# Order of the work where an output product hands over to the first gate product

## The chip, the cores and the metric

The kernel runs on one core of a Trainium2 chip. A core has five engines with queues of their own: TensorE (PE, matrix products; its weight loads are shown as PEld), VectorE (DVE), ScalarE (ACT), GpSimd (POOL) and SyncE (SP, which here issues most DMAs). PE, DVE, ACT and POOL each take their instructions in the order in which they were queued. The metric is the device time of one execution in microseconds (us), the median of several runs; lower is better.

## The reference

A trunk of two layers over 1024 tokens of width 1024, all in float32. Layer 0 mixes tokens by attention, layer 1 by a gated recurrence; each layer ends with a SwiGLU feed-forward block of inner width 2816. Every sub-layer is `x = x + RMSNorm(f(RMSNorm(x)))`. Cut to what matters here:

```python
def rmsnorm(x, g):
    y = x * rsqrt(mean(x * x, axis=-1) + 1e-6)
    return y * g

for layer in range(2):
    m = mixer(rmsnorm(x, norm_mix_pre[layer]))            # ends with ... @ w_out
    x = x + rmsnorm(m, norm_mix_post[layer])
    h = rmsnorm(x, norm_ffn_pre[layer])
    f = (silu(h @ w_gate) * (h @ w_up)) @ w_down
    x = x + rmsnorm(f, norm_ffn_post[layer])
```

The place of this study is the passage from `@ w_out` over the two norms to the first columns of `h @ w_gate`. It comes twice, once in each layer; the text calls each a joint.

## The kernel before, in words

**Precision.** A float32 operand is split into a rounded part (hi, written by a cast on ACT) and the rest (lo, a subtraction on DVE); a product is three matmuls, hi·hi, hi·lo and lo·hi.

**Output product** (`out_product`, matmuls on L602). The 1024 tokens are eight tiles of 128. Tiles 0 to 2 are accumulated together, then 3 to 5, then 6 and 7. When the sums of a tile are complete in PSUM, its norm follows (`norm`, `post_norm_of`, `rstd`, `pre_norm`):

- ACT squares and sums the tile (L179), POOL makes the factor of the norm in two one-column operations (L183 adds the epsilon, L184 is the power -1/2), DVE multiplies by the gain (L251, which reads PSUM) and adds the residual (L257).
- Of the new x, ACT takes the squares again (L179), POOL makes the second factor (L183, L184), and ACT scales (L213). That last instruction is called `scaled` in the code.
- PE turns the scaled tile: eight 128x128 transposes (L223) into two PSUM banks.

**The turned tile** is taken by `HiddenS.take`: ACT copies both banks to SBUF (L85). The feed-forward products go by Strassen's scheme in Winograd's form, seven products in place of eight, so their right-hand operands are seven blocks: three of the turned tile itself and four differences `tf`. They are kept in three groups: the first has two blocks (operands 0 and 1), the second one block (operand 2), the third the four differences (operands 3 to 6). Each group is cast by ACT (L96, hi) and subtracted by DVE (lo); all DVE operations of `take` go through one helper and show as L89. There is one buffer for `tf`.

**The first gate product** (`first`, `strassen`, matmuls on L759 to L761). Tiles 0 to 3 are turned well before tiles 6 and 7 are normed. So the first 256 columns of the first gate block (seven products A11, A12, S2, S3, S1, S4, A22 of twelve 256-column matmuls each) are computed from tiles 0 to 3 while tiles 6 and 7 are normed and turned. The operands of A11 and A12 are those of the first group, S4's that of the second, the others are of the third. `strassen` is a generator: `out_product` takes the products up to a yield, queues a tile's transposes behind the last matmul so far, and the rest of the products behind the transposes (`hold`). Then the late half, columns 256 to 512, needs tiles 4 to 7. L765 to L776 add the products up as they come out of PSUM.

**Its weights** (`gate_load`): the loads (L714), a scaling by the norm's gain on ACT (L717), then sums and differences on DVE (L736 to L738, L743), and for each of the seven a cast on ACT (L729) and a lo part on DVE (L730). S3, S1, the difference L743 and S4 are under `self.behind(behind)`.

**What sets the order.** `self.behind([i, ...])` queues the instructions traced in its block behind instruction i, if they run on i's engine; it adds no wait between engines. For the rest, the program builder plans the order on each queue from dependencies, from the order in which the code issues the instructions, and from a timing of its own; then data dependencies become waits on semaphores.

Of the kernel before, what the change touches and what calls it, by code (L numbers as in the profile page):

```python
# [8 lines left out]
F32 = mybir.dt.float32  # L9
# [27 lines left out]
class HiddenT:  # L37
# [7 lines left out]
    def take(self, t, pst, scratch, pool):  # L45
        nc = self.nc
        if isinstance(t, tuple):
            r, a = t
            hh, hl = (h.rearrange("p k (a t r i) -> p k a t r i", a=2, t=2, r=2)[:, :, a % 2, :, r, :]
                      for h in self.half[a // 2])  # L50
            pst = [ps.rearrange("p a (t i) -> p a t i", t=2) for ps in pst]
        else:
            tok = slice((t % 4) * P, (t % 4) * P + P)
            hh, hl = (h[:, :, tok] for h in self.half[t // 4])
        for q, ps in enumerate(pst):
            hi = hh[:, 4 * q:4 * q + 4]
            self.last = nc.scalar.copy(hi, ps).ins
            self.last_lo = nc.vector.tensor_tensor(
                hl[:, 4 * q:4 * q + 4], ps, hi.bitcast(F32), op=ALU.subtract).ins


class HiddenS:
# [18 lines left out]
    def take(self, t, pst, scratch, pool):  # L81
        nc = self.nc
        hf = scratch.rearrange("p (q a b) -> p q a b", q=2, a=4)
        for q, ps in enumerate(pst):
            nc.scalar.copy(hf[:, q], ps)  # L85
        lo, hi = slice(0, 64), slice(64, P)
        b11, b12, b21, b22 = hf[:, 0, :, lo], hf[:, 0, :, hi], hf[:, 1, :, lo], hf[:, 1, :, hi]
        tf = pool.tile([P, 4, 4, 64], F32, tag="tf", bufs=1, name=self.uid("tf"))
        sub = lambda o, x, y: nc.vector.tensor_tensor(o, x, y, op=ALU.subtract)  # L89
        sub(tf[:, 0], b12, b11)  # L90
        sub(tf[:, 2], b22, b12)
        sub(tf[:, 1], b22, tf[:, 0])
        sub(tf[:, 3], tf[:, 1], b21)
        cols = slice(64 * t, 64 * t + 64)
        for src, (h, l) in zip((hf[:, :, :, lo], hf[:, 1:2, :, hi], tf), self.g):
            self.last = nc.scalar.copy(h[:, :, :, cols], src).ins  # L96
            self.last_lo = sub(l[:, :, :, cols], src, h[:, :, :, cols].bitcast(F32)).ins


class Trunk:  # L100
# [165 lines left out]
    def attention(self, x_src, xT_src, w_v, w_qk, bias_t, o_dst, hT, pools, open_first):  # L266
        nc, tc = self.nc, self.tc
        with ExitStack() as ctx:
# [255 lines left out]
            for q in range(2):  # L524
                wv.append(self.split(None, 4, 256, raw=raws[q]))
                for c in range(2):
                    take(c, (q,))
                    for tt in range(2):
                        v_part(banks[2 * c + tt], wv, 2 * c + tt, range(4 * q, 4 * q + 4))
            squares(0); squares(1)  # L530
            evacuate(vt, 0)
            take(2)
            v_tile(grp, wv, vt, 2)
            squares(2); squares(3)
            evacuate(vt, 1)
            take(3)
            v_tile(grp, wv, vt, 3)
            spread(0)
# [34 lines left out]
    def psum(self):  # L573
        return self.pp.tile([P, 512], F32, tag="mm", bufs=6, name=self.uid("ps"))
# [4 lines left out]
    def out_product(self, ap, pp, first, aT, w, x_src, x_dst, gpost_v, sink, kts):  # L579

        nc = self.nc
# [16 lines left out]
        def matmuls(ps, passes, first, last):  # L598

            for n in range(2):  # L600
                for i, (x, y) in enumerate(passes):
                    self.matmul = nc.tensor.matmul(ps[:, n * 512:(n + 1) * 512], x, y[:, n, :], start=first and i == 0,  # L602
                                     stop=last and i == len(passes) - 1).ins

        def norm(t, ps):
            mg = ap.tile([P, D], F32, tag="mg", bufs=3, name=self.uid("mg"))

            x = self.apool.tile([P, 1152], F32, tag="first", name=self.uid("x"))[:, :D] if t in (2, 5) else None
            return self.post_norm_of([(slice(0, D), ps)], mg, x_src, x_dst, t, gpost, sink, ap, x)
# [6 lines left out]
        for t0 in (0, 3):  # L616
# [30 lines left out]
            last_m = self.last_m  # L647
# [27 lines left out]
        for t in range(2):  # L675
            for i in range(4):

                with self.behind([self.matmul] + ([self.turned[3 + i]] if t == 0 and i < 3 else [])):
                    matmuls(pst[t], [(acts[i][:, t * P:(t + 1) * P], rows[i])], False, i == 3)
            if t == 0:  # L680
                rest = norm(6, pst[0])
                last_m = self.last_m
                turn6 = rest(True)
                squared, summed = self.squared, self.summed


        last, products, hold = first([*last_m, summed], psum)
        with self.behind([squared]):
            rest = norm(7, pst[1])
        last_m = self.last_m  # L690
# [56 lines left out]
    def strassen(self, hS, psum, c, q, cols, behind=()):  # L747

        nc = self.nc
        s1, u2, u3, c22 = c

        def product(name, i):
            ps, a = psum(), q[name]
            for kt in range(4):
                bh, bl = hS.op(i, 0, kt, cols), hS.op(i, 1, kt, cols)
                with self.behind(behind):
                    nc.tensor.matmul(ps, a[:, 0, kt, :], bh, start=kt == 0, stop=False)  # L759
                nc.tensor.matmul(ps, a[:, 0, kt, :], bl, start=False, stop=False)  # L760
                self.matmul = nc.tensor.matmul(ps, a[:, 1, kt, :], bh, start=False, stop=kt == 3).ins  # L761
            return ps

        tt = nc.vector.tensor_tensor
        nc.scalar.copy(s1, product("A11", 0))  # L765
        yield self.matmul
        p2 = product("A12", 1)
        tt(u2, product("S2", 4), s1, op=ALU.add)
        tt(s1, p2, s1, op=ALU.add)
        tt(u3, product("S3", 5), u2, op=ALU.add)  # L770
        p5 = product("S1", 3)
        tt(u2, p5, u2, op=ALU.add)
        yield self.matmul
        tt(c22, p5, u3, op=ALU.add)
        tt(u2, product("S4", 2), u2, op=ALU.add)
        tt(u3, u3, product("A22", 6), op=ALU.subtract)  # L776

    def gate_up(self, ap, hS, early, wg, wu, gain, gO):
# [17 lines left out]
        for j in range(NF // 2):  # L796
            if j == 0:
                cg = blocks()
                strassen([o[:, late] for o in cg], q, late)
                for i, o in enumerate(cg):  # L800
                    nc.scalar.activation(o[:, early], first[:, i], AF.Silu)
                    nc.scalar.activation(o[:, late], o[:, late], AF.Silu)
            else:
                q = self.gate_load(ap, wg, gain, j, ["w"] * 7, self.last if j == 1 else None)
                cg = blocks()
                strassen(cg, q, full)
                for o in cg:
                    nc.scalar.activation(o, o, AF.Silu)
            qu = self.gate_load(ap, wu, gain, j, ["w"] + ["w2"] * 6, hS.last if j == 0 else None)
            cu = blocks()  # L810
            strassen(cu, qu, full)
            for o, u in zip(cg, cu):
                tt(o, u, o, op=ALU.mult)
            a11, a21, a12, a22 = cg
            s1, s2, s4, _ = cu
            tt(s1, a21, a22, op=ALU.add)
            tt(a21, a11, a21, op=ALU.subtract)
            tt(s2, s1, a11, op=ALU.subtract)
            tt(s4, a12, s2, op=ALU.subtract)
            for name, o in (("A11", a11), ("S2", s2), ("S3", a21), ("S1", s1), ("A22", a22),  # L820
                            ("S4", s4), ("A12", a12)):
                nc.sync.dma_start(gO[name][:, j] if name == "A12" else gO[name][j], o)
# [464 lines left out]
```

## Time and profile before

| | us |
|---|---|
| median of 3 runs | 2181.53 |
| lowest and highest of them | 2178.12, 2184.14 |
| the profiled execution, its own time | 2188.6 |
| its span, first to last instruction | 2186.8 |

Mean granted PE clock in the profiled execution: 0.996 of full speed. The two joints lie at about 572 to 599 us and 1540 to 1568 us of the span.

How to read the rows: in a timeline a row is the start, the length, the engine, the line of the code, the operation, output<-inputs with their shape, and in brackets how long the engine had stood idle before and what released it. Rows of several equal instructions are merged (x8). In a view of waits a row is the waiting engine, tile and line, what it waited for, us in total, number of times and the longest. In a view of windows a row gives the length of the window, then busy us with the number of instructions for PE, PEld, DVE, ACT and POOL, then the granted clock, the DMA share and GB/s. SPq is SyncE's queue. Buffer names: `ps` sums in PSUM, `mg` and `x` the tile in its norm, `pst` the transposes, `hS` the groups, `q` and `raw` gate or up weights, `rs` and `ss` the norm's factor and its sum.

### The profile page before, as it was taken

Reading aid. Unit: us, or ns where it says so; the run is one execution under the profiler, and the core shown is the slowest. Engines: PE = TensorE matmul, PEld = TensorE weight load, DVE = VectorE, ACT = ScalarE, POOL = GpSimd, SP = SyncE. Lnnn points to the kernel's source line nnn. Section 1 sums busy time; section 2 is a strip of 40 time slices with the busy share of each in tenths; the row PEclk is TensorE's granted clock in tenths of the full one; section 3 lists DMA queues with packets and bytes.
Section 4 is the critical chain, followed back from the end, with each engine's and each line's share of the span. In section 5 each row is a group of like instructions: output and inputs, shape, how many; then the busy total and the mean of one; then the engine's idle time right before and its main releaser. Section 6 shows DMA issues by size and latency. Waiting matters only on the chain.

```text
span 2186.8 us, 30432 instructions
## 1 busy us (share of the span) xinstructions
PE 2158.0 (99%) x11140; PEld 1803.8 (82%) x11140; DVE 1500.0 (69%) x2458; ACT 1173.2 (54%) x2174; POOL 220.4 (10%) x398
## 2 busy tenths in 40 slices
PE   9999999999999999999999999999999999999998
PEld 8888989878788888888887777887788888888886
DVE  5747555656877677767778667437786767758675
ACT  7656555556755445433446576537755454424452
POOL 2111113121100000000002333102100000000011
PEclk9999999999999999999999999999999999999999
DMA  7111012126334233336467311356133333328565
GB/s 284 44 49 49 30 40 64 43 99 205 133 103 133 92 118 99 106 106 242 136 196 225 98 49 54 95 199 230 63 130 102 121 97 98 110 87 293 169 183 154
DMA packets 167453, 269.42 MB, mean 123 GB/s; under 512 B 13964, under 2 KB 94860, under 8 KB 167304
## 3 DMA queue, kind: packets, MB, share of 16 engines
q1 hardware_dynamic: 166520, 265.38, 37.9%
q10 hardware_dynamic: 784, 2.10, 0.3%
q8 instruction: 87, 1.43, 0.3%
q14 instruction: 62, 0.51, 0.1%
HBM read 199.80 MB, written 65.54 MB: 121 GB/s over the span
## 4 chain that ended last, share of the span: by engine, by line
PE 86%; DVE 5%; ACT 3%; DMA 2%; issue 2%; POOL 1%; SPq 0%; POOLq 0%; DVEq 0%; ACTq 0%
PE ps L760 13%; PE ps L759 13%; PE ps L761 13%; PE ps L602 6%; PE ps L845 5%; PE ps L846 5%; PE ps L844 5%; PE pso L370 3%; PE tr L435 3%; PE psq L167 3%; PE psq L168 2%; PE psq L169 2%; PE ps L168 2%; PE ps L169 2%; PE ps L167 2%
## 5 line engine op out<-in xcount | busy, mean ns | idle before, releaser
L759 PE MATMUL ps<-hS,q 128*128 128x512 f32 (+1 forms) x1288 | 490.4, 381 | 0.0
L760 PE MATMUL ps<-hS,q 128*128 128x512 f32 (+1 forms) x1288 | 489.9, 381 | 0.5 <-DVE hS L89 0.5
L761 PE MATMUL ps<-hS,q 128*128 128x512 f32 (+1 forms) x1288 | 489.2, 380 | 0.0
L730 DVE TENSOR_TENSOR q<-raw,q 128x512 fp32r<-128x512 f32 x308 | 205.6, 688 | 180.7 <-ACT q L729 180.1
L760 PEld LDWEIGHTS ps<-hS,q 128*128 128x128 f32 x1288 | 243.1, 189 | 47.0 <-DVE hS L89 0.9
L761 PEld LDWEIGHTS ps<-hS,q 128*128 128x128 f32 x1288 | 243.0, 189 | 46.1
L759 PEld LDWEIGHTS ps<-hS,q 128*128 128x128 f32 x1288 | 242.7, 189 | 46.1 <-DVE tf L89 0.2
L729 ACT CAST q<-raw 128x512 fp32r<-128x512 f32 x308 | 178.8, 619 | 165.4 <-DVE raw L738 127.6
L845 PE MATMUL ps<-o,o 128*128 128x512 f32 x616 | 240.2, 390 | 0.5 <-DVE o L840 0.4
L846 PE MATMUL ps<-o,o 128*128 128x512 f32 x616 | 237.7, 389 | 0.0
L717 ACT ACTIVATE raw<-raw,gcol 128x256 f32<-128x256 f32 x352 | 150.8, 502 | 138.7 <-DMA raw<-in_ffn_w_up_dram 74.8
L844 PE MATMUL ps<-o,o 128*128 128x512 f32 x616 | 218.6, 390 | 1.8 <-ACT o L839 1.8
L839 ACT CAST o<-raw 128x512 fp32r<-128x512 f32 x173 | 104.2, 622 | 148.3 <-PE ps L846 52.5
L183 POOL TENSOR_SCALAR rs<-ss 128x1 f32<-128x1 f32 x52 | 34.0, 654 | 1416.2 <-ACT junk L179 1344.1
L840 DVE TENSOR_TENSOR o<-raw,o 128x512 fp32r<-128x512 f32 x173 | 116.1, 688 | 53.1 <-ACT o L839 52.6
L844 PEld LDWEIGHTS ps<-o,o 128*128 128x128 f32 x616 | 115.3, 188 | 27.2 <-ACT o L839 3.7
L845 PEld LDWEIGHTS ps<-o,o 128*128 128x128 f32 x616 | 115.6, 188 | 25.6 <-DVE o L840 1.8
L846 PEld LDWEIGHTS ps<-o,o 128*128 128x128 f32 x616 | 115.6, 188 | 24.0
L157 DVE TENSOR_TENSOR wlo<-raw,whi 128x1024 fp32r<-128x1024 f32 x76 | 93.4, 1229 | 58.6 <-ACT whi L156 57.3
L423 DVE TENSOR_TENSOR_SCAN pr<-pr,zero 128x128 f32<-128x128 f32 (+7 forms) x64 | 86.6, 1359 | 51.3 <-POOL pr L420 49.6
L156 ACT CAST whi<-raw 128x1024 fp32r<-128x1024 f32 x76 | 79.8, 1052 | 52.1 <-PE ps L168 23.4
L167 PE MATMUL psq<-hT,whi 128*128 128x512 f32 x256 | 102.4, 400 | 1.2 <-ACT v L310 1.0
(208 smaller groups left out, 4278.6 us busy)
## 6 DMA issues: line engine op xcount, KB each, us to landing
raw<-in_ffn_w_gate_dram SPq DMA_DIRECT2D x44, 512.0 KB, 4.2
raw<-in_ffn_w_up_dram SPq DMA_DIRECT2D x44, 512.0 KB, 4.2
gS<-c SPq DMA_DIRECT2D x88, 256.0 KB, 3.8
raw<-gS SPq DMA_DIRECT2D x88, 256.0 KB, 2.8
gA<-c SPq DMA_DIRECT2D x66, 256.0 KB, 3.4
raw<-gA SPq DMA_DIRECT2D x44, 256.0 KB, 2.7
t<-in_ffn_w_down_dram SPq DMA_DIRECT2D x22, 512.0 KB, 6.5
raw<-in_ffn_w_down_dram SPq DMA_DIRECT2D x41, 256.0 KB, 4.8
```

What stands on the lines that cost most here:

```text
L167: nc.tensor.matmul(ps, wh[:, kt, cols], hh[:, kt, :], start=kt == 0, stop=False)
L602: self.matmul = nc.tensor.matmul(ps[:, n * 512:(n + 1) * 512], x, y[:, n, :], start=first and i == 0, stop=last and i == len(passes) - 1).ins
L717: nc.scalar.activation(raw[:, i], raw[:, i], AF.Copy, scale=gain[:, 4 * k + i:4 * k + i + 1])
L729: self.last = nc.scalar.copy(t[:, 0], src).ins
L730: self.last_lo = nc.vector.tensor_tensor(t[:, 1], src, t[:, 0].bitcast(F32), op=ALU.subtract).ins
L759: nc.tensor.matmul(ps, a[:, 0, kt, :], bh, start=kt == 0, stop=False)
L760: nc.tensor.matmul(ps, a[:, 0, kt, :], bl, start=False, stop=False)
L761: self.matmul = nc.tensor.matmul(ps, a[:, 1, kt, :], bh, start=False, stop=kt == 3).ins
L840: tt(t[:, 1], src, t[:, 0].bitcast(F32), op=ALU.subtract)
L844: nc.tensor.matmul(ps, a[0], b[:, 0], start=first, stop=False)
L845: nc.tensor.matmul(ps, a[0], b[:, 1], start=False, stop=False)
L846: self.matmul = nc.tensor.matmul(ps, a[1], b[:, 0], start=False, stop=last).ins
```

## The change

Three edits.

1. In `HiddenS.take` the first and the second group are issued ahead of the four subtractions that make the differences, the third group after them. The operations are the same.
2. In the last part of `out_product` the scaling of tile 6 (`scaled`) joins the list behind which `gate_load` queues the casts of S3, S1 and S4.
3. In `strassen` the product A12 is issued ahead of the first yield, so that tile 6's transposes are queued behind two products, not one. Between the turns of tiles 6 and 7 then lie S2, S3 and S1.

```diff
@@ HiddenS.take
+        cols = slice(64 * t, 64 * t + 64)
+
+        def group(src, g):
+            h, l = g
+            self.last = nc.scalar.copy(h[:, :, :, cols], src).ins
+            self.last_lo = sub(l[:, :, :, cols], src, h[:, :, :, cols].bitcast(F32)).ins
+
+        group(hf[:, :, :, lo], self.g[0])
+        group(hf[:, 1:2, :, hi], self.g[1])
         sub(tf[:, 0], b12, b11)
         sub(tf[:, 2], b22, b12)
         sub(tf[:, 1], b22, tf[:, 0])
         sub(tf[:, 3], tf[:, 1], b21)
-        cols = slice(64 * t, 64 * t + 64)
-        for src, (h, l) in zip((hf[:, :, :, lo], hf[:, 1:2, :, hi], tf), self.g):
-            self.last = nc.scalar.copy(h[:, :, :, cols], src).ins
-            self.last_lo = sub(l[:, :, :, cols], src, h[:, :, :, cols].bitcast(F32)).ins
+        group(tf, self.g[2])
@@ out_product
-                squared, summed = self.squared, self.summed
+                squared, summed, scaled = self.squared, self.summed, self.scaled
...
-        last, products, hold = first([*last_m, summed], psum)
+        last, products, hold = first([*last_m, summed, scaled], psum)
@@ strassen
         nc.scalar.copy(s1, product("A11", 0))
+        p2 = product("A12", 1)
         yield self.matmul
-        p2 = product("A12", 1)
```

## The prediction

> **What bounds the kernel now.** I read the page first: its busy shares and the chain that ended last.
>
> ```profile
> PE 2158.0 (99%) x11140; PEld 1803.8 (82%) x11140; DVE 1500.0 (69%) x2458; ACT 1173.2 (54%) x2174; POOL 220.4 (10%) x398
> PE 86%; DVE 5%; ACT 3%; DMA 2%; issue 2%; POOL 1%; SPq 0%; POOLq 0%; DVEq 0%; ACTq 0%
> ```
>
> TensorE (PE) is busy 99% of the span and the chain runs on it for 86%. No matmul is removed, so only PE's own gaps can be won. The second view is what PE waited for, longest first (us in total, times, longest).
>
> ```profile
> PE pst L223 <- ACT mg L213: 5.0, 2, 2.8
> PE pst L223 <- ACT mg L85: 1.8, 1, 1.8
> PE ps L760 <- DVE hS L89: 0.5, 2, 0.2
> ```
>
> The first row is the largest wait of the kernel: twice, the transposes (L223) of a tile wait for that tile's scaling (L213). The third view, PE in order of time, shows that both are tile 6 at the end of an output product, just after the product A11 of the first gate (start, length in us; the last A11 matmul, the transposes, and then the first matmul of each joint that runs at the old pace again).
>
> ```profile
> 574.03 0.28 PE L761 MATMUL ps<-hS,q 128*128 128x256 f32 x1
> 576.47 1.97 PE L223 MATMUL pst<-ident,mg 128*128 128x128 f32 x8 [2.16 <-ACT mg L213]
> 579.91 0.28 PE L761 MATMUL ps<-hS,q 128*128 128x256 f32 x1
> ...
> 1542.36 0.28 PE L761 MATMUL ps<-hS,q 128*128 128x256 f32 x1
> 1545.47 1.69 PE L223 MATMUL pst<-ident,mg 128*128 128x128 f32 x8 [2.83 <-ACT mg L213]
> 1549.40 0.28 PE L759 MATMUL ps<-hS,q 128*128 128x256 f32 x1
> ...
> 1553.71 1.03 PE L223 MATMUL pst<-ident,mg 128*128 128x128 f32 x8
> 1554.50 0.36 PE L759 MATMUL ps<-hS,q 128*128 128x256 f32 x1
> 1554.70 0.28 PE L760 MATMUL ps<-hS,q 128*128 128x256 f32 x1
> 1554.82 0.28 PE L761 MATMUL ps<-hS,q 128*128 128x256 f32 x1
> ```
>
> The last four rows are tile 7's turn, with no wait ahead of it: 0.79 us of transposes, 0.20 to the second matmul, then 0.12 us a matmul. A 256-column product of 12 matmuls therefore costs 1.44 us, and an unhindered turn 0.87.
>
> Now the loss at each joint. **Idle:** after the last A11 matmul the next could start 0.12 later, at 574.15 and 1542.48; the transposes start at 576.47 and 1545.47. That is 2.32 + 2.99 = 5.31 us. **Slow stretch:** in the first joint the ninth matmul behind the transposes starts 3.44 us after them (579.91); at full pace it would be 0.79 + 0.20 + 7 x 0.12 = 1.83. In the second joint the thirteenth starts after 3.93 (1549.40) in place of 2.31. That is 1.61 + 1.62 = 3.23 us. The granted clock explains it:
>
> ```profile
> 1526.94 1.14 PE L223 MATMUL pst<-ident,mg 128*128 128x128 f32 x8 [1.77 <-ACT mg L85]
> ...
> 576.40:579.90 3.50, 3.43 (x16) 3.43 (x17) 2.34 (x2) 3.23 (x6) 0.00 (x0) 0.51 0.70 265
> 1527.00:1530.70 3.70, 3.70 (x20) 2.30 (x21) 3.70 (x10) 3.70 (x7) 0.00 (x0) 1.00 0.55 225
> ```
>
> The first row is the 1.8 us wait of the second view; the others are windows, with the clock in the third column from the end: 0.51 behind the 2.2 us wait, 1.00 behind the 1.8 us one. So a wait of 1.8 us cost no clock here and one of 2.2 did.
>
> **Why the scaling is late.** The chain of tile 6 at the first joint, from its residual sum (L257) to its scaling, with what lies beside it; last the same POOL row and its release in the second joint:
>
> ```profile
> 569.47 1.28 DVE L257 SCALAR_TENSOR_TENSOR x<-mg,rs,x 128x1024 f32<-128x1024 f32 x1
> 570.78 1.06 ACT L179 ACTIVATE mg<-x 128x1024 f32<-128x1024 f32 x1 [0.68 <-DVE x L257]
> 571.84 0.60 ACT L729 CAST q<-raw 128x512 fp32r<-128x512 f32 x1
> 572.54 0.69 DVE L730 TENSOR_TENSOR q<-raw,q 128x512 fp32r<-128x512 f32 x1
> 573.14 0.42 DVE L89 TENSOR_TENSOR tf<-mg,tf 128x256 f32<-128x256 f32 x1
> 572.02 2.56 POOL L183 TENSOR_SCALAR rs<-ss 128x1 f32<-128x1 f32 x1 [3.89 <-ACT mg L179]
> 572.98 1.02 ACT L179 ACTIVATE junk<-ps 128x1024 bf16<-128x1024 f32 x1 [0.53 <-PE ps L602]
> 574.42 1.22 DVE L251 TENSOR_TENSOR mg<-ps,g 128x1024 f32<-128x1024 f32 x1
> 574.67 0.57 POOL L184 TENSOR_TENSOR rs<-rs,neghalf 128x1 f32<-128x1 f32 x1
> 575.27 1.15 ACT L213 ACTIVATE mg<-x,rs 128x1024 f32<-128x1024 f32 x1 [1.17 <-POOL rs L184]
> 575.32 0.22 POOL L183 TENSOR_SCALAR rs<-ss 128x1 f32<-128x1 f32 x1
> 576.58 1.05 ACT L96 CAST hS<-tf 128x1024 fp32r<-128x1024 f32 x1
> ...
> 1541.03 2.56 POOL L183 TENSOR_SCALAR rs<-ss 128x1 f32<-128x1 f32 x1 [4.07 <-ACT mg L179]
> 1543.42 1.22 DVE L251 TENSOR_TENSOR mg<-ps,g 128x1024 f32<-128x1024 f32 x1
> ```
>
> The same one-column POOL operation (L183) takes 0.22 us for tile 7 and 2.56 for tile 6, in both joints alike, and both times it ends about 0.16 us after VectorE (DVE) starts L251, the first operation in a while with a PSUM input. Before that DVE ran SBUF-to-SBUF operations back to back, three of them the weights' L730. I read this as POOL being shut out of SBUF: 2.3 us of tile 6's chain. The Trainium skill (SBUF — State Buffer, Who interferes with whom) says that a VectorE instruction with two SBUF inputs blocks a GpSimd one that reads SBUF, for the whole instruction; the trace agrees and shows more, one block of 2.56 us across several instructions.
>
> **The change, part by part.** *A12 ahead of tile 6's transposes.* One 1.44 us product fills the wait. Its operands are ready: the weights A12 were cast with A11's, and it reads the same first group. Left of the idle are 0.88 and 1.55 us if the scaling doesn't move; below 1.8 I take no slow stretch. So this part alone is worth 2 x 1.44 + 3.23 = 6.1 us. PE does no more work; the products behind it move up.
>
> *Casts of S3, S1, S4 behind tile 6's scaling.* On ScalarE (ACT) three casts of 0.6 us go behind L213, and their three L730 on DVE follow them. DVE then has, between L257 (ends 570.75) and L251, only the subtraction L743 (of L730's shape, 0.69) and four small ones of tile 5 (0.42 each, started 0.34 apart): about 2 us, so it falls idle near 572.8 and POOL finishes near 573.6. ACT next has tile 7's square (the L179 at 572.98, when PE ends tile 7). L213 can run at about 574.0 and end at 575.2, before A12 ends at 575.6. In the second joint the same steps end L213 near 1543.7, against A12's end at 1543.9. There tile 5's cast of its third group (1.05 us) may slip ahead on ACT. Left of the wait: nothing to 0.9, nothing to 1.55; I take 0.15 and 0.45.
> The moved casts are due later: S3 is the second product behind the turn, 575.6 + 0.87 + 1.44 = 577.9, and its cast and difference end about 1.3 us behind L213, 576.5 to 578.3 if L257 or L89 comes between. I allow 0.5 us over both joints, 0 to 1.5 as bounds. On SyncE's queue the up weights' load waits for S3's buffer:
>
> ```profile
> 571.98 0.38 SPq L714 DMA_DIRECT2D raw<-in_ffn_w_up_dram  x1
> ...
> 591.23 3.31 ACT L717 ACTIVATE raw<-raw,gcol 128x256 f32<-128x256 f32 x8
> ```
>
> It would go out some 5 us later, still 14 us ahead of its first use, and the store of tile 7's rows behind it on that queue is read only in the stage after next: both hidden.
>
> *First groups of a turned tile first.* DVE does the same ten operations of a tile in another order; the third group's difference ends no later. It pays where PE waits for them, tile 7's first group in the late half of A11:
>
> ```profile
> 588.45 0.28 PE L759 MATMUL ps<-hS,q 128*128 128x256 f32 x1
> 588.96 0.39 PE L760 MATMUL ps<-hS,q 128*128 128x256 f32 x1 [0.23 <-DVE hS L89]
> 589.18 0.28 PE L761 MATMUL ps<-hS,q 128*128 128x256 f32 x1
> ```
>
> 0.51 + 0.22 in place of 0.24 is 0.49 us, in the second joint the same by the second view's "0.5, 2": 0.98 in all. Next late is the third group of tile 7, and behind its cast on ACT the scaling of the up weights (591.23), which PE needs after the late half's seven products; the 0.5 allowed covers that too.
>
> *What is late next: tile 7.* With A12 ahead, only S2, S3, S1 lie between the turns. Tile 7's transposes are then due at 575.6 + 0.87 + 3 x 1.44 = 580.8, and at 1549.1. Now they are not pressed:
>
> ```profile
> 581.11 1.15 ACT L213 ACTIVATE mg<-x,rs 128x1024 f32<-128x1024 f32 x1 [0.18 <-POOL rs L184]
> 584.70 1.03 PE L223 MATMUL pst<-ident,mg 128*128 128x128 f32 x8
> ...
> 1549.83 1.15 ACT L213 ACTIVATE mg<-x,rs 128x1024 f32<-128x1024 f32 x1 [0.18 <-POOL rs L184]
> ```
>
> Its scaling ends at 582.26 and 1550.98, 1.5 and 1.9 us too late. It comes sooner by what tile 6's chain gains (about 1.2), and later by what the moved casts take of ACT (up to 1.8) where they go first. I take a wait of 0.7 us at each joint, bounds 0 and 5.6 (below).
>
> **Sum.** 5.31 + 3.23 + 0.98 = 9.5 us can be won; 0.6 left at tile 6, 1.4 at tile 7 and 0.5 elsewhere go off: 7.0. The profiled execution took 2188.6 us (span 2186.8), so 2181.6 by its own time. The three runs have the median 2181.5; I take the difference from it: **2174.5**, with 2172 to 2177 as this case's own range.
>
> **Rivals.** *The wait moves to tile 7 in full* (0.20). The L730 moved now lie where tile 7's second L183 runs, and L183 has been seen blocked by such operations. [...] If tile 7's scaling ends no sooner than now, PE waits 1.5 + 1.9 = 3.4 in place of 1.4: 5.0 won, 2176.5. For it: three casts ahead of tile 7 on ACT. Against: S2's and A12's evacuations, with PSUM inputs, fall between the L730 and let POOL through.
> *Only the filling works* (0.15). Tile 5's four subtractions hold POOL until L251 anyway, or ACT takes another cast first: the wait left at tile 6 is 0.88 + 1.55, tile 7's about 0.9, the first groups gain nothing: 6.1 - 0.9 = 5.2, 2176.3. The order on each queue is planned when the program is built, so an edit can also come out as no new order at all.
> *Slower* (0.04). Tile 7's scaling is later than now by the casts (1.8) and a full block (2.56 - 0.22 = 2.3): PE waits 1.5 + 4.1 = 5.6 and 6.0 us, long enough for the slow clock (3.2 again). 11.6 + 3.2 + 1.1 - 9.5 is 6.4 lost: 2187.9. It turns into a loss when tile 7's wait passes 2.6 us a joint, which means a scaling about 1 us later than now.
>
> **How the numbers follow.** The forecast has 0.61. 0.3% is 6.5 us, about what a measurement tells from no change, so faster means under 2175.0. The forecast's 2174.5 lies just beyond it: of its 0.61 I count 0.44 as faster, and 0.06 of the two middle rivals, whose terms are uncertain by 2 us. Of the slower case half lies beyond 0.3%. Faster 0.50, within 0.48, slower 0.02. The range takes in all but the slow rival and the outermost values: 2171 to 2180.
>
> **What would show it.** Right: A12's matmuls ahead of both first turns, the transposes of tile 6 with under 1 us of idle, clock 1.00 behind them, L183 of tile 6 under 1.5 us, no wait for L89 in the late A11. Wrong: a slow stretch behind tile 7's turn, L183 of tile 7 over 1 us, a PE wait for the q of S3 or S1, or a longer wait at 1526.9, where the new order of tile 4's operations could move that 1.8 us wait either way.

## The result, and the profile after

The kernel after the change takes **2192.69 us** (median; 2189.44 to 2193.62) against **2181.78 us** (2178.12 to 2184.14) before: a ratio of 1.0050 with the interval 1.0038 to 1.0063. It is slower by 10.9 us, 0.5%. The prediction was 2174.5 with a range of 2171 to 2180: the forecast said faster, and the time lies above its range. The profiled execution after took 2193.62 us, its span is 2191.8.

The view of waits after, PE's rows in the joints (us in total, times, longest). The change moves the matmuls of `strassen` from L759 to L765, the copy of A11 from L765 to L771, the transposes from L223 to L229, the scaling from L213 to L219. It is the first edit that adds these six lines, so the runs below that leave it out keep the old numbers:

```profile
PE ps L765 <- ACT first L771: 7.3, 2, 3.6
...
PE ps L765 <- DVE first L780: 1.9, 2, 1.0
PE pst L229 <- ACT mg L85: 1.8, 1, 1.8
```

The wait of the transposes for tile 6's scaling (5.0 in two before) is gone, as the prediction wanted. In its place stands a longer one that it did not name: twice 3.6 us, a matmul of the gate waits for `first`, the SBUF copy of the product A11. PE in order of time shows which matmul (start, length; the idle time in brackets): the first and the last matmul of A11, then the first of A12, the turns of tiles 6 and 7, a late wait, and the first matmul of the down product, which ends the stage; then the second joint.

```profile
573.00 0.68 PE L765 MATMUL ps<-hS,q 128*128 128x256 f32 x1
...
574.72 0.28 PE L767 MATMUL ps<-hS,q 128*128 128x256 f32 x1
...
578.63 0.58 PE L765 MATMUL ps<-hS,q 128*128 128x256 f32 x1 [3.63 <-ACT first L771]
581.36 1.25 PE L229 MATMUL pst<-ident,mg 128*128 128x128 f32 x8
585.32 1.04 PE L229 MATMUL pst<-ident,mg 128*128 128x128 f32 x8
590.10 0.38 PE L765 MATMUL ps<-hS,q 128*128 128x256 f32 x1 [0.88 <-DVE first L780]
...
1001.58 0.39 PE L850 MATMUL ps<-o,o 128*128 128x512 f32 x1
...
1543.73 0.68 PE L765 MATMUL ps<-hS,q 128*128 128x256 f32 x1
...
1549.36 0.58 PE L765 MATMUL ps<-hS,q 128*128 128x256 f32 x1 [3.63 <-ACT first L771]
1561.94 0.39 PE L765 MATMUL ps<-hS,q 128*128 128x256 f32 x1 [1.02 <-DVE first L780]
...
1973.41 0.39 PE L850 MATMUL ps<-o,o 128*128 128x512 f32 x1
```

The product that was to fill the wait stands in one itself, and tile 6's turn, queued behind it, comes later than if nothing had been put ahead of it. ACT over the same time says why the copy is late:

```profile
574.67 1.14 ACT L219 ACTIVATE mg<-x,rs 128x1024 f32<-128x1024 f32 x1
575.72 0.61 ACT L735 CAST q<-raw 128x512 fp32r<-128x512 f32 x1
576.22 1.05 ACT L94 CAST hS<-tf 128x1024 fp32r<-128x1024 f32 x1
577.17 1.14 ACT L735 CAST q<-raw 128x512 fp32r<-128x512 f32 x2
578.21 0.37 ACT L771 COPY first<-ps 128x256 f32<-128x256 f32 x1
```

The scaling, then the three moved casts (L735) with tile 5's cast (L94) among them, and only then the copy of A11, 3.2 us after A11's last matmul ended. And the waits cost clock (windows: length, busy us of the five engines, granted clock third from the end):

```profile
578.60:582.20 3.60, 3.57 (x18) 3.57 (x19) 1.75 (x3) 2.11 (x3) 1.28 (x2) 0.56 0.92 270
...
1549.30:1553.60 4.30, 4.25 (x20) 4.25 (x21) 1.78 (x3) 2.63 (x5) 1.29 (x2) 0.50 0.97 278
```

Why A12 needs that copy at all stands in the instruction order of the two programs (matmuls and transposes on PE's queue since A11's first, output<-inputs, the columns of the PSUM tile that are written, what it waits for; the number behind `ps` is the PSUM tile):

```
before   0 L759 MATMUL ps_6437<-hS_5513,q_6393 columns   0 to 255 [waits DVE]          first matmul of A11
        32 L759 MATMUL ps_6437<-hS_5513,q_6394 columns 512 to 767 [waits Activation]   first matmul of A12
after    0 L765 MATMUL ps_6437<-hS_5513,q_6393 columns   0 to 255 [waits DVE]
        12 L765 MATMUL ps_6437<-hS_5513,q_6394 columns 512 to 767 [waits Activation]
```

A11 and A12 write two parts of one PSUM tile, and A12 waits for the ACT instruction that reads A11's part out. It did so before the change too; then tile 6's turn and S2 lay between the products, and nothing of it showed. The two parts share no column: the wait is a semaphore that the program builder put there, and no run here shows that the chip needs it.

### The profile page after: what moved, and what is told of

It reads as the page before. It is cut to its first block, busy times and chain, and to the rows that moved or that the text cites. A ratio compares the mean times of both kernels' runs of the same rounds, so it can differ in the third digit from the quotient of the medians.

```text
span 2191.8 us, 30418 instructions
## 1 busy us (share of the span) xinstructions
PE 2157.4 (98%) x11140; PEld 1804.1 (82%) x11140; DVE 1501.1 (68%) x2458; ACT 1170.9 (53%) x2174; POOL 216.5 (10%) x398
## 3 DMA queue, kind: packets, MB, share of 16 engines
q8 instruction: 87, 1.43, 0.3%
## 4 chain that ended last, share of the span: by engine, by line
PE 87%; DVE 4%; ACT 3%; DMA 2%; issue 2%; POOL 1%; SPq 0%; POOLq 0%; ACTq 0%; DVEq 0%
PE ps L765 13%; PE ps L767 13%; PE ps L766 13%; PE ps L608 8%; PE ps L850 5%; PE ps L851 5%; PE ps L852 5%; PE pso L376 3%; PE tr L441 3%; PE psq L173 3%; PE psq L174 2%; PE psq L175 2%; PE ps L174 2%; PE ps L175 2%; PE ps L173 2%
## 5 line engine op out<-in xcount | busy, mean ns | idle before, releaser
L765 PE MATMUL ps<-hS,q 128*128 128x512 f32 (+1 forms) x1288 | 491.2, 382 | 9.2 <-ACT first L771 7.3
L765 PEld LDWEIGHTS ps<-hS,q 128*128 128x128 f32 x1288 | 243.0, 189 | 56.2 <-ACT first L771 7.7
L735 ACT CAST q<-raw 128x512 fp32r<-128x512 f32 x308 | 178.1, 616 | 169.2 <-DVE raw L744 132.3
L189 POOL TENSOR_SCALAR rs<-ss 128x1 f32<-128x1 f32 x52 | 30.6, 589 | 1426.4 <-ACT junk L185 1354.5
```

What stands on the lines that cost most here:

```text
L735: self.last = nc.scalar.copy(t[:, 0], src).ins
```

## The experiments

Three theories came out of this (the expectation of a single run may number its own otherwise). **Theory 1:** the whole loss is A12's wait for A11's copy; it needs two edits together, the early A12, which exposes the wait, and the moved casts, which push the copy back. **Theory 2:** the new order of a turned tile's groups has a share in it. **Theory 3**, on the missing gain: the execution that the prediction read was slow in its joints, and a usual one had little to give.

As a measure of a joint I take the time from A11's first matmul to the first matmul of the down product, read from PE's timeline as in the rows above: after, 1001.58 - 573.00 = 428.58 and 1973.41 - 1543.73 = 429.68 us; before, in the profiled execution of the prediction, 426.56 and 427.24. This measure takes in some 400 us of gate and up products behind the hand-over, so that all of a delay is in it; no slow stretch of any run's joint lies behind its first 14 us. All runs, with the ratio to runs of the kernel before on the same chip:

| kernel | joint 1 | joint 2 | median us | ratio (interval) |
|---|---|---|---|---|
| `before_again` | 423.72 | 423.72 | 2180.17 | 0.9992 (0.9980 to 1.0004) |
| `before_third` | 423.72 | 423.72 | 2179.36 (one run) | |
| `groups_only` (edit 1) | 425.02 | 423.72 | 2179.98 | 1.0001 (0.9993 to 1.0010) |
| `casts_only` (edit 2) | 425.22 | 425.22 | 2182.03 | 1.0009 (1.0000 to 1.0017) |
| `a12_only` (edit 3) | 423.81 | 423.81 | 2179.04 | 0.9997 (0.9988 to 1.0006) |
| `groups_a12` (1, 3) | 423.80 | 428.33 | 2182.76 | 1.0001 (0.9988 to 1.0014) |
| `casts_a12` (2, 3) | 428.74 | 428.88 | 2191.00 | 1.0042 (1.0029 to 1.0055) |
| `all_three` (after) | 428.75 | 429.86 | 2191.14 | 1.0049 (1.0035 to 1.0063) |
| `own_bank` (all, own tiles) | 424.56 | 424.55 | 2180.44 | 0.9999 (0.9990 to 1.0008) |
| `copy_on_dve` (all, copy on DVE) | 424.35 | 424.34 | 2182.60 | 0.9998 (0.9986 to 1.0011) |
| `own_bank_a12` (1, 3, own tiles) | 426.75 | 425.83 | 2185.04 | 1.0023 (1.0012 to 1.0033) |

### The change again, and each edit alone

`all_three` is the kernel after, on the chip of the other three.

> The changed kernel once more, beside the kernel before. Theory 1: A12 is written into the second half of the PSUM tile whose first half holds A11, so it waits until ScalarE has copied A11 out (L771), and that copy stands on ScalarE behind tile 6's scaling and the three casts moved there; the two joints of the first trace are 2.0 and 2.5 us longer than before, so this run should be about 4.5 us slower. Theory 2: the moved casts alone cost the time: the same number. Theory 3: the order elsewhere in the kernel costs most of it (the medians differ by 10.9 us, the joints by 4.5): 9 to 12 us slower.

The same joints and the same two waits came again. The kernel was 10.8 us slower (2191.14 against 2180.34), which is the number of that text's theory 3, not the 4.5 us of theories 1 and 2. The 4.5 came from the prediction's execution of the kernel before, whose joints turn out below to have been long. Against joints of 423.72 us, those of `all_three` are longer by 11.2 us in all, so that the order elsewhere in the kernel isn't needed for the loss.

`a12_only` has only this:

```diff
+        p2 = product("A12", 1)
         yield self.matmul
-        p2 = product("A12", 1)
```

> A12 ahead of the first yield alone. Theory 1: A12 still waits for the copy of A11, which stands behind the scaling alone, so it takes the place that the transposes had: PE idle 2.5 us a joint in place of 2.3, slow stretch kept, 0 to 1 us slower than before. Theory 2: without the casts behind the scaling A12 fills the wait: 4 to 6 us faster.

PE in its first joint, A12 and the turn of tile 6:

```profile
573.89 0.39 PE L759 MATMUL ps<-hS,q 128*128 128x256 f32 x1 [1.14 <-ACT first L765]
575.43 1.03 PE L223 MATMUL pst<-ident,mg 128*128 128x128 f32 x8
```

A12 waits already here, but for 1.14 us only, since on ACT the copy follows the scaling directly. The turn waits no longer. One wait has taken the place of the other and the time is unchanged. Theory 1 was right on the kind of wait and wrong on its size (2.5 us and a slow stretch); theory 2's gain of 4 to 6 us did not come.

`casts_only` has only the second edit:

```diff
-        last, products, hold = first([*last_m, summed], psum)
+        last, products, hold = first([*last_m, summed, scaled], psum)
```

> The casts of S3, S1 and S4 behind the scaling alone, A12 where it was. Theory 1: the scaling ends about 2.8 us behind A11's first matmul (as in the changed kernel's trace) in place of 4.1 and 4.8, PE's wait ahead of tile 6's transposes falls to about 1 us, the slow stretch goes: 4 to 6.5 us faster, less what S1 and S3 wait for their weights. Theory 2: the casts are what costs: 3 us or more slower.

Its joints are 1.5 us longer than those of `before_again`; the ratio can hardly be told from none. Neither theory's number came: not 4 to 6.5 us faster, and by the medians 1.7 us slower, not 3. Its turns of tiles 6 and 7, with 0.87 and 0.36 us of wait:

```profile
575.31 1.09 PE L223 MATMUL pst<-ident,mg 128*128 128x128 f32 x8 [0.87 <-ACT mg L213]
582.77 1.09 PE L223 MATMUL pst<-ident,mg 128*128 128x128 f32 x8 [0.36 <-ACT mg L213]
```

Moving the casts did not bring the scaling forward: it starts 1.67 us after A11's first matmul, as in `before_again`. Neither edit alone costs anything near 10.9 us.

### The shared tile taken away

In `own_bank` all three edits stay, and the joints' first six products take three PSUM tiles in turn: A12 no longer writes into A11's.

```diff
-            halves = []
+            tiles, n = [], [0]
             def psum():
-                if not halves:
-                    ps = new_psum()
-                    halves.extend([ps[:, 512:768], ps[:, 0:256]])
-                return halves.pop()
+                i, n[0] = n[0], n[0] + 1
+                if i < 3 or i == 6:
+                    tiles.append(new_psum())
+                return tiles[i % 3 if i < 6 else 3][:, 512 * (i // 3 % 2):512 * (i // 3 % 2) + 256]
```

> All three edits, and the first gate's products take three PSUM tiles in turn, so that A12 no longer shares one with A11. Theory 1: A12 starts right behind A11, the wait for L771 is gone at both joints, the transposes of tile 6 follow with under 0.5 us of idle and the clock stays at 1.00: 6 to 9 us faster than before, less a wait of up to 1.5 us a joint ahead of tile 7's transposes. Theory 2: the wait stays at tile 6 or moves to S3 or S1: within 2 us of the changed kernel.

A12's first matmul no longer waits for ACT. In its first joint neither A12 nor tile 6's turn waits; the next wait is that of a later product, now the second one of A12's tile, for the reading of A12 (L775):

```profile
575.78 1.04 PE L229 MATMUL pst<-ident,mg 128*128 128x128 f32 x8
...
581.25 0.39 PE L765 MATMUL ps<-hS,q 128*128 128x256 f32 x1 [1.41 <-DVE first L775]
```

The joints are 4.2 and 5.3 us shorter than those of `all_three`, and the loss is gone. The 6 to 9 us of gain that theory 1 added did not come (2180.44, ratio 0.9999); theory 2 falls. The copy of A11 is as late as after, behind the three casts:

```profile
574.18 1.14 ACT L219 ACTIVATE mg<-x,rs 128x1024 f32<-128x1024 f32 x1
...
577.72 0.37 ACT L771 COPY first<-ps 128x256 f32<-128x256 f32 x1
```

So a late copy costs 10.9 us only where A12 has to wait for it. One thing more differs: the planner put S3 ahead of tile 7's turn again (36 matmuls between the two turns, 24 after the change), here and in the next run. A joint of `groups_a12` below parts the two: S3 stands ahead of tile 7's turn there, and A12's longer wait with the slow clock behind it makes that joint 4.5 us longer than the run's other one.

### The copy taken out from behind the casts

`copy_on_dve` keeps the edits and the shared tile, and copies A11 in the joints by another engine:

```diff
-        nc.scalar.copy(s1, product("A11", 0))
+        (nc.vector.tensor_copy if isinstance(behind, list) else nc.scalar.copy)(s1, product("A11", 0))
```

> All three edits and the shared PSUM tile, but in the two joints A11's copy is done by DVE, where it stands between the two DVE operations of tile 6 ahead of its scaling's product, not by ACT behind the casts. Theory 1 (it is the time of that copy that A12 waits for): the wait falls from 3.6 to about 1.5 us, the slow clock goes with it, 2179 to 2183 us. Rival (A12's early place costs by itself, whenever the copy comes, for instance by the turns that it pushes back): 2188 us or more with no such wait.

The copy on DVE's timeline:

```profile
575.02 0.41 DVE L771 COPY first<-ps 128x256 f32<-128x256 f32 x1
```

PE's timeline, A12's first matmul and tile 6's turn:

```profile
575.49 0.38 PE L765 MATMUL ps<-hS,q 128*128 128x256 f32 x1 [1.43 <-DVE first L771]
577.02 1.03 PE L229 MATMUL pst<-ident,mg 128*128 128x128 f32 x8
```

A12 starts 0.06 us after that copy ends. The wait falls from 3.63 to 1.43, there is no slow clock in the joints, and the loss is gone: the rival, that an early A12 costs by itself, falls. The forecasts of theory 1 (a wait of about 1.5, 2179 to 2183 us) were met.

### Which edits are needed

`casts_a12` has edits 2 and 3, `groups_a12` 1 and 3.

> Edits on the casts and on A12 together, the order of a turned tile's groups as before. Theory 1 (A12 writes the second half of A11's PSUM tile and so waits for the copy of A11, which the moved casts push back on ACT): a wait of A12 for that copy of about 3.6 us in each joint, slow clock behind it, 2189 to 2192 us, 9 to 11 above the kernel before. Theory 2 (the new order of the groups takes part in the loss, by the engines that it fills): no more than half of that, 2181 to 2186 us.

> Edits on the groups and on A12 together, the casts where they were. Theory 1: A11's copy stands right behind tile 6's scaling on ACT again, A12 waits some 1.1 us for it, no slow clock in the joints, 2177 to 2180 us. Theory 2 (the groups' new order costs by itself): 2183 us or more.

`casts_a12` shows the two waits in full, and 2191.0 us:

```profile
578.01 0.39 PE L759 MATMUL ps<-hS,q 128*128 128x256 f32 x1 [3.64 <-ACT first L765]
...
1544.65 0.39 PE L759 MATMUL ps<-hS,q 128*128 128x256 f32 x1 [3.63 <-ACT first L765]
```

So the order of the groups is not needed for the loss, and theory 2 falls. `groups_a12` has the ratio 1.0001; its median, 2182.76, is above theory 1's 2177 to 2180, on a chip where the kernel before took 2181.58. Its first joint is as forecast, its second is not: 428.33 us. POOL's timeline there:

```profile
1535.53 2.56 POOL L189 TENSOR_SCALAR rs<-ss 128x1 f32<-128x1 f32 x1 [4.07 <-ACT mg L185]
```

ACT's, the scaling and the copy behind it:

```profile
1538.78 1.15 ACT L219 ACTIVATE mg<-x,rs 128x1024 f32<-128x1024 f32 x1 [1.81 <-POOL rs L190]
1539.83 0.35 ACT L771 COPY first<-ps 128x256 f32<-128x256 f32 x1
```

PE's, the first matmul of A12:

```profile
1540.24 0.58 PE L765 MATMUL ps<-hS,q 128*128 128x256 f32 x1 [3.10 <-ACT first L771]
```

Here POOL was held up for 2.56 us, the scaling came late, the copy behind it too, and A12 waited 3.10 us: the same wait by another cause. With A12 early, whatever delays tile 6's scaling on ACT also delays A11's copy, and with it a product that has nothing to do with tile 6.

`groups_only` was to complete the table.

> The order of a turned tile's groups alone, A12 and the casts as before. Theory 1 (the loss needs A12 ahead of the turns and the moved casts together): no wait at A12, 2178 to 2183 us, within 0.1% of the kernel before; joints near 424 us unless POOL is held up in one of them. Theory 2 (the order of the groups costs by itself): 2184 us or more.

As theory 1 had it, but for a plainer reason. The built program is that of the kernel before on all five queues, instruction for instruction, addresses and waits included: the planner puts those operations where it did. The same holds beside the other edits: `groups_a12` is the program of `a12_only`, and the kernel after is that of `casts_a12`. So edit 1 changes nothing in any combination run here, and it is edits 2 and 3 together that move S3 behind tile 7's turn (`casts_a12` has it there too). `groups_only` is therefore a fourth profile of the kernel before, and `casts_a12` a third one of the kernel after.

### The kernel before, looked at again

> The kernel before, unchanged, for a second profiled execution. Theory 3 (the execution that the prediction was read from was slow in the joints: slow clock at one of tile 6's two waits in each, POOL held up for over 2 us): this one, near the median of 2181, shows joints (A11 to the first down product) near 424 us in place of 427, with POOL's copy of the sums done in under 1 us and with slow clock behind at most one of the waits. Rival (the joints always hold these 2.6 us): 426 to 427 us again.

> The kernel before once more, one profiled execution. Theory 3: joints of about 423.7 us with POOL's copy of the sums under 1 us, or, if POOL is held up in one of them, about 426 us or more in that one. Rival: a joint above 426 us without POOL held up.

Both joints of both take 423.72 us, on two chips. First the view of waits of `before_again`, where the prediction had found 5.0 us:

```profile
PE pst L223 <- ACT mg L213: 1.8, 2, 0.9
```

POOL's timeline, 2.56 us in the prediction's execution:

```profile
571.83 0.35 POOL L183 TENSOR_SCALAR rs<-ss 128x1 f32<-128x1 f32 x1 [3.90 <-ACT mg L179]
```

ACT's, the scaling and the copy of A11:

```profile
573.80 1.14 ACT L213 ACTIVATE mg<-x,rs 128x1024 f32<-128x1024 f32 x1
574.84 0.36 ACT L765 COPY first<-ps 128x256 f32<-128x256 f32 x1
```

PE's, from A11's first matmul to the first of the down product, with all that waited between:

```profile
572.13 0.68 PE L759 MATMUL ps<-hS,q 128*128 128x256 f32 x1
...
574.99 1.09 PE L223 MATMUL pst<-ident,mg 128*128 128x128 f32 x8 [0.88 <-ACT mg L213]
...
585.93 0.39 PE L760 MATMUL ps<-hS,q 128*128 128x256 f32 x1 [0.23 <-DVE hS L89]
995.85 0.39 PE L844 MATMUL ps<-o,o 128*128 128x512 f32 x1
```

POOL is not held up, the scaling runs as soon as ACT has squared tile 7, PE waits 0.88 us, and the clock stays at 1.00. `before_third` agrees (waits of 0.88 and 0.23 in the first joint). `groups_only`, the same program, had one joint of the other kind. On POOL's timeline:

```profile
570.35 2.56 POOL L189 TENSOR_SCALAR rs<-ss 128x1 f32<-128x1 f32 x1 [3.89 <-ACT mg L185]
```

And on PE's:

```profile
574.80 1.09 PE L229 MATMUL pst<-ident,mg 128*128 128x128 f32 x8 [2.17 <-ACT mg L219]
```

Over four profiles of this program, three of eight joints were held up, two of them in the execution that the prediction read. Theory 3 holds, on these few profiles: the two held-up joints were 2.84 and 3.52 us longer than 423.72, which is 6.4 of the 8.4 us between that execution and the median of `before_again`.

### A version that beats both?

`own_bank_a12` has edits 1 and 3 and the products' own tiles as in `own_bank`; the casts stay where they were.

> Candidate for a version that beats both kernels: order of the groups and A12 ahead of the turns, casts where they were, the joints' products in PSUM tiles of their own. Theory 1: no wait at A12, tile 6's scaling done before A12 ends, so that what is left is the wait of a later product for an evacuation, up to 1.4 us; joints of 423 to 424.6 us, 2177 to 2181 us. Theory 3 says that the kernel before has only about 1.1 us a joint to give in an execution near its median, so at most 2 us are won. Rival (0.9 us of wait and 1.4 us of filling in each joint are won as the prediction counted): joints of 421.5 us or less, 2176 us or less.

It is slower, by 0.23%: 2185.04 us is above theory 1's range and far from the rival's, and theory 3's "at most 2 us are won" was not put to the test. The profiled execution (2189.04) is the longest of its seven. POOL was held up in its first joint, but in both the costly wait is the later product's, and it is followed by the slow clock. PE in the first joint:

```profile
582.31 0.38 PE L765 MATMUL ps<-hS,q 128*128 128x256 f32 x1 [1.83 <-DVE first L775]
```

The window behind it:

```profile
582.30:586.10 3.80, 3.79 (x19) 3.79 (x20) 2.27 (x4) 1.38 (x3) 0.00 (x0) 0.55 0.01 4
```

The second joint has the same wait, 1.84 us, and a slow stretch behind it. The reading of A12 stands on DVE behind tile 6's subtractions, and the next product of that tile waits for it. No version here beats the kernel before.

## Why the prediction was wrong

**The failed step.** "Its operands are ready: the weights A12 were cast with A11's, and it reads the same first group." The operands were; the place of the result was not. In this program a matmul also waits for its PSUM tile, and A12's is A11's, to be read out by ACT first: 3.63 us at each joint. The kernel before shows no such wait, since the products stood apart; it would have been seen in `first`, which hands out the halves of one tile, and in the semaphore of A12's first matmul. From there the second edit turns against the first: "three casts of 0.6 us go behind L213" puts them ahead of A11's copy on the same queue. The text asked what was queued behind the casts for tile 7's sake, and not for A11's.

The Trainium skill (Perfetto Trace Analysis, Optimizing Tensor Performance, Matmuls) says that independent matmul groups should rotate through PSUM banks so that the reading of one overlaps the matmuls of the next. By the Trainium skill (PSUM — Partial Sum Buffer, Specifications) a bank holds 512 float32 values, so columns 0 and 512 of a tile are two banks. The trace agrees with the aim (`own_bank`, no wait at A12) and shows its limit: another bank of the same tile did not do, A12 waited 3.63 us.

**The sum.** Against `before_again`, the joints after are longer by 428.58 - 423.72 = 4.86 and 429.68 - 423.72 = 5.96, together 10.8 of the 10.9 us measured. In joint 1, 3.63 + 0.88 us of wait stand for 0.88 + 0.23, which is 3.4; in joint 2, 3.63 + 1.02 for the same, 3.5. The rest, 1.5 and 2.4, fits the stretches at half clock: half of what is left of each behind the wait is (3.41 - 0.25) / 2 = 1.6 and (6.83 - 1.60) / 2 = 2.6.

**The size of the gain.** "I take the difference from it" carried the gaps of a 2188.6 us execution over to a median of 2181.5. Of the 9.5 us to be won, `before_again` has 2 x 0.88 of wait and 2 x 0.49 in the late half of A11: 2.7, and no slow clock. With that alone the forecast would have been near 2179, no change to be measured. That the profiled execution lay above all three timed runs (2184.14 the slowest) was in front of me.

**POOL and the casts.** The reading was right that POOL is held up there, and after, POOL's L189 of tile 6 takes 0.42 us. It does so in all twelve joints of the runs with the casts moved, while five of the fourteen without have 2.56 us. But nothing was gained from it where POOL was not held up before either: the scaling starts 1.67 us after A11's first matmul after (574.67 - 573.00), and just as long after it in `before_again` (573.80 - 572.13). What holds it then is ACT's square of tile 7, which ends as the scaling starts (ACT's timeline of `before_again`):

```profile
572.79 1.02 ACT L179 ACTIVATE junk<-ps 128x1024 bf16<-128x1024 f32 x1 [0.54 <-PE ps L602]
```

**The first groups.** 0.98 us was counted; the edit left every queue as it was, and both waits of 0.23 us stayed in `groups_only`. Its rival, "no new order at all", happened to this edit. After the change these waits are gone, as the prediction's sign of being right wanted, but not by this edit: `a12_only` has none either, and `own_bank`, with all three edits, has both.

**Tile 7.** 0.7 us a joint was counted, and none came. Between the turns lie S2 and S1 alone, not also S3 as the section on the change had it, since the planner put S3 behind tile 7's turn; and A12's wait pushes that turn back. Both turns after run without a wait. The late wait for L780 (0.88 and 1.02) was not foreseen: S4, written to the second part of S1's tile, waits for the reading of S1, which needs S3.

**The rivals.** The slower one (2187.9) had the sign, and 6.4 us of loss where 10.9 came, by luck: its mechanism, tile 7's late scaling, did not occur.

## What to carry to other kernels

Before a matmul is moved up, look at where it writes as well as at what it reads: which tile, who reads that tile's last content, and what stands ahead of that reader on its queue, above all what the same change puts there. An operation that is moved "out of the way" on one engine lands ahead of everything that was queued behind its new place. Where the profiled execution lies outside the timed runs, take a second profile before counting its gaps as gains. And where a planner sets the order, see first whether an edit changes the built program at all.

## What the runs showed of the hardware

**The clock works by a fixed grid of windows.** The clock records of the traces (start of a stretch at half clock in a joint, its length, and PE's wait ahead of it; some of the joints):

```
before         576.43  3.41   wait 574.31 to 576.47
before        1545.82  3.41   wait 1542.64 to 1545.47
after          578.38  3.41   wait 575.00 to 578.63
after         1547.76  6.83   wait 1545.73 to 1549.36
groups_a12    1539.05  6.83   wait 1537.14 to 1540.24
all_three      577.84  3.41   wait 572.82 to 576.45
own_bank_a12   582.70  3.41   wait 580.48 to 582.31
own_bank_a12  1552.09  3.41   wait 1549.05 to 1550.89
groups_only    none           wait 572.63 to 574.80
```

Stretches are 3.41 us long or twice that, and their starts within an execution lie a whole number of 3.4133 us apart (1545.82 - 576.43 = 969.39 = 284 x 3.4133). So the same wait may cost clock or not: the 1.83 us of `own_bank_a12` lie within one window, and half clock followed; the 2.17 us of `groups_only`, on the grid drawn back from that trace's last stretch (2171.41), are split into 1.34 and 0.83, and nothing followed. The 1.77 us before 1526.94 in the kernel before, split into 0.17 and 1.60, cost none either. By these rows the limit lies between 1.60 and 1.83 us of idle in a window, about half; that is an estimate. With PE's idle time added up in each of the 8248 windows at full clock of the thirteen traces, half clock followed all 31 that had 1.76 us or more, and none of the 8210 that had 1.61 or less; of the seven between, it followed five. Once at half clock, 1.19 us of idle in the next window (`groups_a12`, 1539.05 to 1540.24) was enough to stay there for a second; 0.30 us (`copy_on_dve`, the window from 1179.43) was not.

The Trainium skill (TensorE: Matmul & The Clock Gate, What's actually happening) gives a free-running window of 3.4 us, with which the grid agrees; its idle window of about 3.4 us as the condition does not fit, since 1.83 us sufficed.

**POOL's hold-up comes and goes in the same program.** The one-column L183 of tile 6 takes 0.35 or 2.56 us. It starts 0.15 us after the same DVE operation in both kinds. DVE's timeline of `groups_a12`, where POOL's row is 1535.53 and 2.56 us:

```profile
1535.38 0.76 DVE L89 TENSOR_TENSOR tf<-mg 128x256 f32<-128x256 f32 x2
```

And of `before_again`, where it is 571.83 and 0.35 us:

```profile
571.68 0.76 DVE L89 TENSOR_TENSOR tf<-mg 128x256 f32<-128x256 f32 x2
```

The short kind ends 0.08 us after the first of these two subtractions (572.10 and 572.18); the long one, as the prediction read it, only behind the start of L251. With the casts moved it was the short kind in all twelve joints, again ending 0.08 us after the subtraction beside it. VectorE's and POOL's timelines of `casts_only`:

```profile
572.07 0.42 DVE L89 TENSOR_TENSOR tf<-mg,tf 128x256 f32<-128x256 f32 x1
572.15 0.42 POOL L183 TENSOR_SCALAR rs<-ss 128x1 f32<-128x1 f32 x1 [3.90 <-ACT mg L179]
```

That the second edit does away with the hold-up is argued from these 26 joints, not shown by a test of its own; why only five of the fourteen with the casts in their old place had it stays open.
